# Cutting the last load before the first store into 16 KB runs, and the first store into a 16 KB and a 48 KB part

## Chip, cores and metric

One core of a Trainium2 chip. The metric is the device time of one execution in microseconds. Most executions of one kernel agree within about 0.3%, single ones lie further off; differences are therefore told as a ratio with a 95% interval, and "faster" or "slower" means by more than 2%.

## The reference

A rotary embedding on half of each head. `x` is (16, 512, 16, 64) in float32, 33.55 MB; the first 32 numbers of each head are rotated with tables `cos` and `sin`, the other 32 pass unchanged.

```python
x1, x2 = x[..., :32], x[..., 32:]
first  = x1[..., :16] * cos[..., :16] - x1[..., 16:] * sin[..., :16]
second = x1[..., :16] * sin[..., :16] + x1[..., 16:] * cos[..., :16]
return concatenate([first, second, x2], axis=-1)
```

The work is small; the 67.1 MB that must be read and written are the problem.

## The kernel before

`x` is seen as four tiles of 8 MiB. In each, a partition holds 16 rows of 4 KB, next to each other in memory, so that a transfer of n rows moves one run of n x 4 KB per partition. The profile counts 16 transfer engines, and each moves eight of the 128 runs of such a transfer. A ring of three tiles in the on-chip memory takes the loads; VectorE rotates in place; the store goes out from the ring.

```python
    def load(t, lo=0, hi=K):                      # K = 16 rows
        nc.sync.dma_start(out=rows(t, lo, hi), in_=xf[t, :, lo * R : hi * R])

    def store(t, lo=0, hi=K):
        nc.sync.dma_start(out=of[t, :, lo * R : hi * R], in_=rows(t, lo, hi))
    # ... stage is set to zero, cos and sin loaded from the GpSimd queue
    load(0, 0, K0)                                # K0 = 4
    load(0, K0, K)
    load(1)
    load(2, 0, KC)                                # KC = 8
    # ... the tables are spread over the partitions on VectorE
    rotate(0, 0, K0)
    rotate(0, K0, (K0 + K) // 2)
    rotate(0, (K0 + K) // 2, K)
    store(0)
    load(2, KC, K)
    load(3)                                       # its ring slot is that of tile 0
    for t in range(1, T):                         # T = 4
        rotate(t, 0, KC)
        rotate(t, KC, K)
        store(t)
```

All loads and stores are issued by the sync engine and stand in one queue. It turns from loading to storing twice: at the first store, and after the load of tile 3.

Of the kernel before, what the change touches and what calls it, by code (L numbers as in the profile page):

```python
# [1 line left out]

# [4 lines left out]


@with_exitstack
def kernel(  # L10
    ctx: ExitStack,
    tc: tile.TileContext,
    x: bass.AP,
    cos: bass.AP,
    sin: bass.AP,
    out: bass.AP,
):
    nc = tc.nc
    fp32 = mybir.dt.float32
    P = 128  # L20
    B, S, H, D = x.shape
    Q = D // 4
    HF = D // 2



    K = 16
    T = B * S // (P * K)
    PB = S // K
    REP = P // PB  # L30
    R = H * D
    NS = 3
    KC = K // 2
    K0 = K // 4

    xf = x.rearrange("b s h d -> (b s h d)").rearrange("(t p f) -> t p f", t=T, p=P)
    of = out.rearrange("b s h d -> (b s h d)").rearrange("(t p f) -> t p f", t=T, p=P)
    cosf = cos.rearrange("(p k) j -> p (k j)", k=K)
    sinf = sin.rearrange("(p k) j -> p (k j)", k=K)

    const_pool = ctx.enter_context(tc.tile_pool(name="const", bufs=1))
    b_pool = ctx.enter_context(tc.tile_pool(name="bp", bufs=1, space=bass.MemoryType.PSUM))


    ring = const_pool.tile([P, NS, K, H, D], fp32)
    stage = const_pool.tile([P, 2, K, HF], fp32)
    spun = const_pool.tile([P, 2 * K, Q], fp32)
    packed = const_pool.tile([PB, 2 * K, Q], fp32)
    table = const_pool.tile([P, 2, K, 2, Q], fp32)

    def rows(t, lo, hi):
        return ring[:, t % NS, lo:hi].rearrange("p k h d -> p (k h d)")

    def load(t, lo=0, hi=K):
# [6 lines that stand above are left out]
    nc.vector.memset(stage[:, :, :, 0:Q], 0.0)  # L61
    spread = stage.rearrange("(j b) t k i -> j b t (k i)", b=REP)
    nc.gpsimd.dma_start(out=spread[:, 0, 0], in_=cosf)  # L63
    nc.gpsimd.dma_start(out=spread[:, 0, 1], in_=sinf)  # L64
    load(0, 0, K0)
    load(0, K0, K)
    load(1)
    load(2, 0, KC)




    PQ = PB // REP
    nc.vector.stream_shuffle(  # L74
        out=spun[:],
        in_=stage.rearrange("p t k j -> p (t k) j")[:, :, 0:Q],
        mask=[j % PQ * REP for j in range(PB)],
    )
    for q in reversed(range(REP)):
        n = PQ * (q + 1)  # L80
        nc.vector.tensor_copy(out=packed[0:n], in_=spun[q * PB : q * PB + n])  # L81

    for r in range(REP):
        nc.vector.tensor_copy(  # L84
            out=table[r * PB : (r + 1) * PB].rearrange("p t k c j -> p (t k) c j"),
            in_=packed.unsqueeze(2).to_broadcast((PB, 2 * K, 2, Q)),
        )
    C = table[:, 0].rearrange("p k c j -> p k (c j)")
    Sn = table[:, 1].rearrange("p k c j -> p k (c j)")

    def rotate(t, lo, hi):
        n = hi - lo
        x1 = ring[:, t % NS, lo:hi, :, 0:HF]
        c = C[:, lo:hi].unsqueeze(2).to_broadcast((P, n, H, HF))
        s = Sn[:, lo:hi].unsqueeze(2).to_broadcast((P, n, H, HF))
        b_full = b_pool.tile([P, KC, H, HF], fp32, name="b_t")
        b_t = b_full[:, 0:n]
        nc.vector.tensor_mul(out=b_t, in0=x1, in1=s)  # L98
        nc.vector.tensor_mul(out=x1, in0=x1, in1=c)  # L99
        nc.vector.tensor_sub(  # L100
            out=x1[:, :, :, 0:Q], in0=x1[:, :, :, 0:Q], in1=b_t[:, :, :, Q:HF]
        )
        nc.vector.tensor_add(  # L103
            out=x1[:, :, :, Q:HF], in0=x1[:, :, :, Q:HF], in1=b_t[:, :, :, 0:Q]
        )

    rotate(0, 0, K0)
    rotate(0, K0, (K0 + K) // 2)
    rotate(0, (K0 + K) // 2, K)
    store(0)  # L110
    load(2, KC, K)
    load(3)
    for t in range(1, T):
# [5 lines that stand above are left out]
# [1 line left out]
_INS = ['x', 'cos', 'sin']  # L120
_OUTS = [((16, 512, 16, 64), 'float32')]


# [23 lines left out]
```

## Time and profile before

| | before |
|---|---|
| time, median of 3 runs | 162.55 us (162.5 to 162.89) |
| span of the profiled run | 160.9 us |
| VectorE busy | 112.9 us (70%) |
| transfer queue busy, of 16 engines' span | 97.7% |
| mean rate over the span | 418 GB/s |

The span is shorter than the time because the time also counts what is around the program. In the lines of the profile, DVE is VectorE, POOL is GpSimd, SPq is the sync engine's queue, and L55 is line 55 of the kernel. The row to look at is the queue: with 97.7% busy, only two things can be gained, the rest of 2.3%, or time in which packets move slowly though they count as busy. The second kind is not to be seen in a busy share.

### The profile page before, as it was taken

What the parts mean: (1) busy time and instruction counts of PE and PEld (TensorE: products, weight loads), DVE (VectorE), ACT (ScalarE), POOL (GpSimd) and SP (SyncE); (2) the same over time, 40 slices, a digit from 0 to 9 for tenths busy, and PEclk for the clock granted to TensorE, in tenths of its full rate; (3) what the DMA queues carried; (4) which work ended last, traced back from release to release, by engine and by line L of the source; (5) the groups of instructions that cost most, each with busy time, mean ns of one, the idle gap of its engine ahead of it and who ended that gap; (6) DMA issues with size and microseconds to landing.
All of it is one profiled execution on the core that took longest, in us unless ns stands there. A gap on an engine that the chain in (4) does not pass through costs nothing.

```text
span 160.9 us, 116 instructions
## 1 busy us (share of the span) xinstructions
DVE 112.9 (70%) x47; POOL 1.4 (1%) x6
## 2 busy tenths in 40 slices
DVE  1049999999999999999999991699999900000000
POOL 3000000000000000000000000000000000000000
DMA  6999999969999996999996996998998998998992
GB/s 195 554 391 391 391 456 521 521 261 521 391 391 261 521 521 261 521 391 391 472 570 261 521 521 261 521 423 358 521 423 358 521 423 358 521 423 358 521 423 98
DMA packets 1504, 67.24 MB, mean 418 GB/s; under 512 B 192, under 2 KB 192, under 8 KB 224
## 3 DMA queue, kind: packets, MB, share of 16 engines
q1 hardware_dynamic: 1440, 67.11, 97.7%
q0 software_dynamic: 64, 0.13, 0.2%
HBM read 33.69 MB, written 33.55 MB: 418 GB/s over the span
## 4 chain that ended last, share of the span: by engine, by line
DMA 50%; DVE 28%; DVEq 1%; issue 0%; SPq 0%
DMA ring<-in_x_dram 31%; DMA out_dram<-ring 18%; DVE b_t L98 10%; DVE ring L99 10%; DVE ring L100 5%; DVE ring L103 3%; DVEq L142 1%; SPq L55 0%; DVEq L98 0%
## 5 line engine op out<-in xcount | busy, mean ns | idle before, releaser
L98 DVE TENSOR_TENSOR b_t<-ring,table 128x4096 f32<-128x4096 f32 (+2 forms) x9 | 35.6, 3959 | 5.4 <-DMA ring<-in_x_dram 5.2
L99 DVE TENSOR_TENSOR ring<-ring,table 128x4096 f32<-128x4096 f32 (+2 forms) x9 | 35.6, 3950 | 0.3
L100 DVE TENSOR_TENSOR ring<-ring,b_t 128x2048 f32<-128x2048 f32 (+2 forms) x9 | 18.4, 2049 | 0.3
L103 DVE TENSOR_TENSOR ring<-ring,b_t 128x2048 f32<-128x2048 f32 (+2 forms) x9 | 18.4, 2042 | 0.0
L74 DVE LOAD_MASK_SELECT spun<-stage x1 | 0.0, 14 | 8.7 <-DMA stage<-in_sin_dram 8.7
L84 DVE COPY table<-packed 32x1024 f32<-32x1024 f32 x4 | 2.7, 684 | 0.1
L81 DVE COPY packed<-spun 32x512 f32<-32x512 f32 (+3 forms) x4 | 1.7, 416 | 0.1
L61 DVE MEMSET stage<- 128x512 f32 x1 | 0.5, 485 | 0.9 <-PEq L131 0.9
L74 DVE STREAM_SHUFFLE spun<-stage 128x512 f32<-128x512 f32 x1 | 0.7, 722 | 0.0
L63 POOL DMA_DIRECT2D stage<-in_cos_dram x1 | 0.6, 649 | 1.3 <-DVE stage L61 1.3
L64 POOL DMA_DIRECT2D stage<-in_sin_dram x1 | 0.5, 532 | 0.0
L131 POOL MEMSET const-bfloat16-1.0<- 128x1 bf16 x1 | 0.1, 96 | 0.0
L131 POOL MEMSET const-float32-0.0<- 128x1 f32 x1 | 0.1, 93 | 0.2 <-issue 0.2
L131 POOL MEMSET const-float32-1.0<- 128x1 f32 x1 | 0.1, 93 | 0.0
L131 POOL MEMSET const-uint8-127<- 128x1 uint8 x1 | 0.1, 93 | 0.0
## 6 DMA issues: line engine op xcount, KB each, us to landing
ring<-in_x_dram SPq DMA_DIRECT2D x2, 4096.0 KB, 44.9
ring<-in_x_dram SPq DMA_DIRECT2D x1, 6144.0 KB, 21.6
ring<-in_x_dram SPq DMA_DIRECT2D x1, 2048.0 KB, 7.7
stage<-in_cos_dram POOLq DMA_DIRECT2D x1, 64.0 KB, 6.3
stage<-in_sin_dram POOLq DMA_DIRECT2D x1, 64.0 KB, 7.7
out_dram<-ring SPq DMA_DIRECT2D x4, 37.2
ring<-in_x_dram SPq DMA_DIRECT2D x2, 34.7
```

Source lines behind the costliest of these rows:

```text
L61: nc.vector.memset(stage[:, :, :, 0:Q], 0.0)
L63: nc.gpsimd.dma_start(out=spread[:, 0, 0], in_=cosf)
L64: nc.gpsimd.dma_start(out=spread[:, 0, 1], in_=sinf)
L74: nc.vector.stream_shuffle(out=spun[:], in_=stage.rearrange("p t k j -> p (t k) j")[:, :, 0:Q], mask=[j % PQ * REP for j in range(PB)],)
L81: nc.vector.tensor_copy(out=packed[0:n], in_=spun[q * PB : q * PB + n])
L84: nc.vector.tensor_copy(out=table[r * PB : (r + 1) * PB].rearrange("p t k c j -> p (t k) c j"), in_=packed.unsqueeze(2).to_broadcast((PB, ...
L98: nc.vector.tensor_mul(out=b_t, in0=x1, in1=s)
L99: nc.vector.tensor_mul(out=x1, in0=x1, in1=c)
L100: nc.vector.tensor_sub(out=x1[:, :, :, 0:Q], in0=x1[:, :, :, 0:Q], in1=b_t[:, :, :, Q:HF])
L103: nc.vector.tensor_add(out=x1[:, :, :, Q:HF], in0=x1[:, :, :, Q:HF], in1=b_t[:, :, :, 0:Q])
L131: nc = _bacc.Bacc("TRN2", target_bir_lowering=False, num_devices=1)
L142: with _tile.TileContext(nc) as tc:
```

## The change

The intent: packets are slow only where the queue turns from loading to storing, so let the packets there be short.

```diff
-    load(2, 0, KC)
+    load(2, 0, K0)
+    load(2, K0, KC)
...
-    store(0)
+    store(0, 0, K0)
+    store(0, K0, K)
```

## The prediction

> **What bounds the kernel now.** I read the page first, for busy shares and the queue, then the chain of waits, then the timeline of issues, then the stretches around the places where the queue turns from loading to storing.
>
> From the page:
>
> ```profile
> span 160.9 us, 116 instructions
> DVE 112.9 (70%) x47; POOL 1.4 (1%) x6
> DMA  6999999969999996999996996998998998998992
> ...
> q1 hardware_dynamic: 1440, 67.11, 97.7%
> ...
> HBM read 33.69 MB, written 33.55 MB: 418 GB/s over the span
> ```
>
> The reader should see that VectorE has 30% to spare and the transfer queue has 2% to spare: its packets took 97.7% of what 16 engines have in 160.9 us. The sixes in the row of tenths are not idle time; a packet is booked where it starts, and one of 64 KB lasts longer than half a slice. The 67.11 MB cannot shrink, because the change neither adds nor drops a byte. So only two things in the queue can move the time: engine time that is idle, and engine time in which a packet moves slower than it could.
>
> The issues, from the timeline (start, length, queue, line):
>
> ```profile
> 0.74 1.89 SPq L55 DMA_DIRECT2D ring<-in_x_dram  x4
> 43.37 0.35 SPq L58 DMA_DIRECT2D out_dram<-ring  x1
> 43.77 29.60 SPq L55 DMA_DIRECT2D ring<-in_x_dram  x2
> 73.46 55.74 SPq L58 DMA_DIRECT2D out_dram<-ring  x3
> ```
>
> Four loads, 20 MiB, are queued at 0.74 us. The first store is issued at 43.37, while the fourth load is still moving, so there is no hole in front of it. The last store is issued at the end of the last stretch, 73.46 + 55.74 = 129.2, and it needs 8.39 MB / 435 GB/s = 19.3 us; as the queue ends near 159.6, its turn comes only at about 140. So VectorE is some 11 us ahead at the end. The chain view says the same in another way: it runs through VectorE up to 128.8 and stops there; its shares (DMA 50%, DVE 28%) are one path of releases and not what limits the rate.
>
> Now the rate, stretch by stretch (from and to, length, busy of VectorE and GpSimd, clock, DMA share, GB/s):
>
> ```profile
> 41.20:48.40 7.20, 7.13 (x4) 0.00 (x0) 1.00 1.01 437
> 48.40:52.40 4.00, 3.97 (x2) 0.00 (x0) 1.00 0.95 262
> 52.40:71.70 19.30, 19.16 (x7) 0.00 (x0) 1.00 1.00 435
> 71.70:81.40 9.70, 9.63 (x3) 0.00 (x0) 1.00 1.00 432
> 81.40:98.30 16.90, 15.62 (x6) 0.00 (x0) 1.00 1.00 434
> 98.30:101.00 2.70, 0.00 (x0) 0.00 (x0) 1.00 1.10 437
> 101.00:120.40 19.40, 18.27 (x6) 0.00 (x0) 1.00 1.01 439
> ```
>
> These are the first six of eight runs per engine of the fourth load (32 KB each), its last two, the first store, the second half of tile 2's load, seven of eight runs of the load of tile 3, its last run, and the second store. Everything goes at 432 to 439 GB/s, but the second line is at 262 with the engines at work for 0.95 of it. In that line 262 x 4.00 = 1048 KB moved, two 32 KB runs on each of 16 engines; they took 0.95 x 4.00 = 3.80 us where 1048 KB / 435 = 2.41 us would do. **The first turn from load to store costs 1.39 us**, in the last two runs of the load and not in the store. The single transfer records of the trace agree: a 32 KB run takes 1.213 us everywhere else, and there, averaged over the engines, the two together took 1.38 us more. At the second turn the line at 98.30 is 16 runs of 64 KB, one per engine, with 1.10 x 2.70 = 2.97 us of records begun in it, of which 0.3 belong to packets on its rim; the records give 0.25 us over 2.418. From store to load (71.70) nothing is lost. The rest of the 2%: about 0.64 us in the very first run, 0.33 us of small gaps while the two table loads pass, and about 3 us ahead of the first byte and after the last.
>
> **What the Trainium skill says.** "DMA: Bandwidth & Descriptors", section "Where 436 GB/s comes from", puts the ceiling at 16 ports x 32 B x 850 MHz = 435.2 GB/s. The trace agrees: 435 in the long store. So no run size can make the undisturbed stretches faster. The same page, section "Why small descriptors are slow (HBM only)", gives a fixed cost of about 3 cycles for each packet; the trace gives a little more for these long runs: 16 KB take 611 ns and 64 KB 2418 ns, so 2418 - 611 = 1807 ns for 48 KB, and 611 - 1807/3 = 9 ns fixed. The same page, section "Two DMAs through the same engine are not ordered", says that descriptors start in order but are pipelined, and that the read and the write side of an engine are separate queues. So while the last load runs are being written, the reads of the store behind them can already be under way; this fits where the loss lies, and is my best reason for it, though no run shows it yet. "SBUF — State Buffer", section "Who interferes with whom", says that a DMA never contends with a compute engine; the trace agrees so far that 32 KB and 64 KB runs hold their time beside a VectorE that is busy 99% (41.20 and 52.40).
>
> **The change part by part.** (1) The load of rows 0 to 7 of tile 2 becomes two transfers of rows 0 to 3 and 4 to 7. On each engine 8 runs of 32 KB become 16 of 16 KB: 8 more x 9 ns = 0.07 us. (2) The first store becomes rows 0 to 3 (8 runs of 16 KB per engine) and rows 4 to 15 (8 of 48 KB) for 8 of 64 KB: again 0.07 us. (3) Two more completion writes per engine at 9 ns, 0.02 us. All of it lies on the path, as the engines are busy to the end: +0.16 us in sum. (4) Issues: the small store needs the first quarter of tile 0 alone, so it may be issued when VectorE is done with that at 22.6 us, but it stands in the same rings behind 20 MiB of loads that end at about 52.8; nothing starts earlier. Two more issues of about 0.4 us on the sync queue fall where it waits anyway. (5) The load of tile 3 now waits for both store parts. They land together with the old end, near 73, and its data are next in the queue only at 81.4: 8 us of slack. VectorE's instructions and their order are the same; its wait of 4.86 us for tile 3 stays and costs nothing, as the 11 us above show. (6) The turn: its 1.39 us now meets 16 KB runs on both sides. That is the one term that can shrink, and the intent of the change.
>
> **The rivals.**
> A. The engine reads ahead by a number of runs. For it: the slow stretch begins on all engines with the last run but one (between 48.73 and 49.00), and at the second turn it is also a whole last run that is slow. Then with 16 KB runs it holds half the bytes and costs half: 1.39 / 2 = 0.70 saved, 0.16 paid, -0.54: 162.0. If it vanished nearly altogether, -1.2: 161.4.
> B. The engine reads ahead by bytes, or the loss is a one-time filling of its buffers at the first store. For it: the second turn, with 64 KB runs, costs 0.25 and not 2.8 us, against what A says of larger runs; two 32 KB runs and one of 64 KB are the same bytes. Then the loss stays, spread over three or four 16 KB runs, and only the 0.16 us are left: 162.7.
> C. VectorE's traffic sets it: it was busy at the first turn and idle (0.00) at the second. Against it stand the skill and the other busy stretches. It gives 162.7 too, as VectorE does the same work at that time.
> D. The earlier issue of the small store opens a hole, or the load of tile 3 is late, so that the store of 19.3 us is not covered. Slack of 8 us speaks against it; it would give 163 or more.
>
> **Range and chances.** B and C together get about 50%, A in its two forms 45%, D and anything unforeseen 5%. The first is at 162.7, the second at 161.4 to 162.0; the middle of this mixture is 162.3. Runs of the kernel before lie between 162.5 and 162.89, so 0.2 us of scatter is added on both sides: 161.4 to 163.0. Two per cent is 3.25 us, more than twice the whole loss at the turn, so faster than that is near impossible, and slower needs a hole in the queue: 1%, 98%, 1%.
>
> **What would show it right or wrong.** Right for A: in the stretch of the last 1 MB of loads before the first store, the changed kernel moves clearly more than 262 GB/s, with a loss of about 0.7 us, and the span is about 160.4. Right for B: about 1.4 us are lost there, over more runs. Everything else should stand still: 432 to 439 GB/s in the other stretches, a second turn of about 0.25 us, store to load without loss, VectorE's 112.9 us and its one wait near 102. I am wrong if the queue has a hole anywhere, if the loss moves to the border between the two store parts, or if the second turn changes along with the first.

## The result, and the profile after

| | before | changed |
|---|---|---|
| median of 4 runs each | 162.72 us (162.5 to 162.97) | 163.01 us (162.78 to 163.19) |
| ratio, 95% interval | | 1.0017 (0.9993 to 1.0041) |

A ratio is the mean time of one kernel's fast runs over that of the other's of the same rounds, so it is not quite the ratio of the medians. The median of 163.01 lies 0.01 above the top of the predicted range; carried to the 162.55 that the prediction started from, the ratio gives 162.83, which lies inside. The point of 162.3 was too low either way.

The page of the changed kernel:

```profile
span 160.6 us, 122 instructions
DVE 112.9 (70%) x47; POOL 1.4 (1%) x6
...
q1 hardware_dynamic: 1728, 67.11, 97.7%
```

VectorE and the share of the queue are as they were; the queue has 288 more packets, the 256 of the cut runs and 32 completion writes. The issues, in the timeline of the changed kernel:

```profile
0.74 2.38 SPq L55 DMA_DIRECT2D ring<-in_x_dram  x5
22.47 21.34 SPq L58 DMA_DIRECT2D out_dram<-ring  x2
43.85 29.36 SPq L55 DMA_DIRECT2D ring<-in_x_dram  x2
73.30 55.54 SPq L58 DMA_DIRECT2D out_dram<-ring  x3
```

The small store is issued at 22.47 us and not at 43.4, as foreseen, and nothing comes earlier for it. Then the rate by stretches of the changed kernel (columns as in the prediction: from and to, length, busy of VectorE and GpSimd, clock, DMA share, GB/s):

```profile
41.20:46.20 5.00, 4.97 (x3) 0.00 (x0) 1.00 0.98 419
46.20:48.40 2.20, 2.17 (x2) 0.00 (x0) 1.00 1.06 454
48.40:52.00 3.60, 3.60 (x1) 0.00 (x0) 1.00 0.96 287
52.00:71.30 19.30, 19.13 (x8) 0.00 (x0) 1.00 1.01 438
71.30:81.00 9.70, 9.63 (x3) 0.00 (x0) 1.00 1.00 432
97.80:100.40 2.60, 0.00 (x0) 0.00 (x0) 1.00 0.94 403
```

The slow stretch is still there, in the same place, with 16 KB runs in it. How much it costs is worked out from such a line in one way throughout this document: share x length is the engines' time for what began in the stretch, GB/s x length the bytes, and bytes / 435 GB/s the time that they need; the difference is the loss. Here 0.96 x 3.60 = 3.46 us for 1033 KB, which need 2.38: **1.08 us**, against 1.39 before. At the second turn it is 0.94 x 2.60 - 1048 / 435 = 0.03, against 0.26 (line 98.30:101.00 of before). The queue of this one trace is thus some 0.4 us shorter and the span 0.3 us, and yet the times do not fall. One of the two must be scatter, and the experiments begin there. (The traced execution was the fastest of the changed kernel's four: its span is 160.6 us, the others' are 160.7, 161.0 and 161.0.)

### The profile page after: what moved, and what is told of

It reads as the page before. It is cut to its first block, busy times and chain, and to the rows that moved or that the text cites. A ratio compares the mean times of both kernels' runs of the same rounds, so it can differ in the third digit from the quotient of the medians.

```text
span 160.6 us, 122 instructions
## 1 busy us (share of the span) xinstructions
DVE 112.9 (70%) x47; POOL 1.4 (1%) x6
## 3 DMA queue, kind: packets, MB, share of 16 engines
q1 hardware_dynamic: 1728, 67.11, 97.7%
## 4 chain that ended last, share of the span: by engine, by line
DMA 50%; DVE 28%; DVEq 1%; issue 0%; SPq 0%
DMA ring<-in_x_dram 31%; DMA out_dram<-ring 18%; DVE b_t L99 10%; DVE ring L100 10%; DVE ring L101 5%; DVE ring L104 3%; DVEq L144 1%; SPq L55 0%; DVEq L99 0%
```

## The experiments

Two theories were left, as the prediction names them. A: the engine reads ahead by a number of runs, so short runs at the turn make it cheap. B: the engine has to get ahead by a number of bytes once, at the first store, whatever the runs. C, VectorE's traffic as the cause, was the third.

| run | what was changed against before | first turn, us lost | later turns | time, ratio to before (95%) |
|---|---|---|---|---|
| (before) | | 1.39 | 0.26 | |
| e1 | nothing | 1.15 | 0.20* | one look: 162.78 against 162.92 |
| (changed) | the change | 1.08 | 0.03 | 1.0017 (0.9993 to 1.0041) |
| e2 | the change again | 1.14 | 0.17* | 1.0018 (0.9993 to 1.0042) |
| e3 | only the load cut | 1.22 | 0.17* | 0.9997 (0.9975 to 1.0019) |
| e4 | only the store cut | 1.31 | 0.32* | 1.0011 (0.9989 to 1.0033) |
| e5 | no rotations | 1.03 | 0.07* | one look: 162.38 against 162.61 |
| e6 | an early small store | 1.18 | 0.09, 0.03* | 1.0025 (1.0007 to 1.0043) |
| e7 | tile 2 loaded whole | 1.10 | 0.09* | 1.0545 (1.0529 to 1.0561) |
| e8 | 4 KB runs before the store | 0.95 | 0.03* | 1.0004 (0.9989 to 1.0019) |
| e9 | 512 B of zeros stored at the start | 1.19 | 0.19* | 1.0017 (1.0002 to 1.0032) |
| e12 | 2 KB of zeros after the first load | 0.30 | 0.36* | 0.9993 (0.9971 to 1.0014) |
| e10 | 4 KB of zeros after the first load | 0.03 | 0.01* | 1.0056 (1.0038 to 1.0074) |
| e11 | stores from a second queue | 1.28 | under 0.1 in all* | 1.1141 (1.1119 to 1.1163) |

Values with a star come from the records of single transfers in the trace (the mean over 16 engines of what a transfer took beyond the usual time of its size), the others from the lines quoted here. Where both were taken they agree within 0.1.

### Is the difference between the two traces one of the kernels?

e1, no edit:

> The unchanged kernel, for a second trace. If what the turns cost is a property of the kernel, the first turn from load to store costs 1.38 us per engine again and the second 0.25, within 0.1. If they wander by 0.3 us from run to run, the drop from 1.38 to 1.04 and from 0.25 to 0.04 that the changed kernel's trace shows is no effect of the change.

The stretch at the first turn, second trace of before:

```profile
48.30:52.30 4.00, 3.96 (x2) 0.00 (x0) 1.00 0.89 262
```

0.89 x 4.00 - 1048 / 435 = 1.15 us. So the same kernel shows 1.39 and 1.15: it wanders by 0.24, more than the 0.1 allowed for, and most of the drop to 1.08 is within this.

e2, the change again, with five rounds:

> The changed kernel again, with more rounds. If the trace is right that the queue itself is 0.4 us shorter (0.34 less at the first turn, 0.21 less at the second, 0.16 more for runs), the ratio is 0.997 to 0.999. If the times are right, 1.001 to 1.003.

```profile
48.00:52.00 4.00, 4.00 (x1) 0.00 (x0) 1.00 1.03 324
```

1.03 x 4.00 - 1296 / 435 = 1.14 us, the value of e1, which was traced on the same chip. The ratio is 1.0018 again, so the times were right and not the single trace. The interval holds 1; that the change costs anything at all is not shown.

### One part alone

e3:

```diff
-    load(2, 0, KC)
+    load(2, 0, K0)
+    load(2, K0, KC)
```

> Only the load in front of the store in 16 KB runs. If the engine reads ahead by runs of the load (A), this alone brings the first turn from 1.38 to about 0.7 to 1.0 us; the store keeps 64 KB runs. If it reads ahead by bytes (B), the first turn stays at 1.2 to 1.5. Fixed cost 0.08 us.

```profile
48.00:52.00 4.00, 4.00 (x1) 0.00 (x0) 1.00 1.03 315
```

1.03 x 4.00 - 1260 / 435 = 1.22 us: above what A allowed (1.0), at the lower edge of B.

e4:

```diff
-    store(0)
+    store(0, 0, K0)
+    store(0, K0, K)
```

> Only the store in 4 and 12 rows, the load keeps 32 KB runs. If the length of the store's runs that are read ahead sets the loss, the first turn falls below 1.1 us here and not in the run with the split load. If the load's runs set it, it stays at 1.38. Fixed cost 0.08 us.

```profile
48.30:52.30 4.00, 3.96 (x2) 0.00 (x0) 1.00 0.94 266
```

1.31 us, not below 1.1. Neither part does what it was made for, and they do not do it together.

### Is it VectorE, or the size of the runs?

e5 leaves out all `rotate` calls, so its result is wrong; the transfers and their order stay.

```diff
-    rotate(0, 0, K0)
-    rotate(0, K0, (K0 + K) // 2)
-    rotate(0, (K0 + K) // 2, K)
...
-        rotate(t, 0, KC)
-        rotate(t, KC, K)
```

> The kernel before without its rotations (a wrong result on purpose): the same transfers in the same order with VectorE idle from about 16 us on. If VectorE's traffic makes the first turn dear (C), its loss falls from 1.38 to 0.3 us or less. If the transfers alone make it (A or B), it stays at 1.2 to 1.5.

```profile
48.00:52.00 4.00, 0.00 (x0) 0.00 (x0) 1.00 0.86 262
52.00:71.30 19.30, 0.00 (x0) 0.00 (x0) 1.00 1.00 435
```

VectorE is at 0.00 and the turn still costs 1.03 us, a little under the forecast of 1.2 and near the lowest of the others; the store behind it runs at the same 435 GB/s. C falls as the main cause; a tenth or two from VectorE could not be told from scatter. The time, 162.38 us without any rotation, also shows how little VectorE has to do with it.

e8, very short runs:

```diff
-    load(2, 0, KC)
+    for r in range(KC):
+        load(2, r, r + 1)
```

> Rows 0 to 7 of tile 2 in eight loads of 4 KB runs before the first store. A by runs: the first turn costs under 0.4 us; the fixed cost is (64 - 8) runs x 9 ns = 0.5 us. B by bytes: 1.0 to 1.5 us over some ten runs.

```profile
48.50:52.20 3.70, 3.70 (x1) 0.00 (x0) 1.00 0.99 319
```

0.95 us, with runs an eighth as long as before. A's forecast of under 0.4 fails; B's 1.0 is missed by 0.05. The 0.5 us that 56 more runs per engine were to cost at 9 ns each would be a ratio of 1.003, which lies outside the measured 0.9989 to 1.0019.

e7, long runs:

```diff
-    load(2, 0, KC)
+    load(2)
...
-    load(2, KC, K)
```

> Tile 2 loaded in one piece before the first store, so the first turn is from 64 KB to 64 KB runs, as the second. A by runs: 2 to 2.8 us at the first turn, or 0.25 if long runs are cheap. B, one-time or by bytes: 1.2 to 1.5 us.

```profile
57.70:61.60 3.90, 3.87 (x2) 0.00 (x0) 1.00 0.90 269
...
139.00:148.80 9.80, 8.89 (x3) 0.00 (x0) 1.00 0.08 33
```

1.10 us with 64 KB runs, 0.1 under B's forecast. So the loss is the same within its scatter for runs of 4, 16, 32 and 64 KB, which is the end of A. That this kernel is 8.9 us slower was not foreseen and has another cause, in the second line: from 139.0 to 148.8 the engines stand still (share 0.08). The load of tile 3 is issued only at 82.06, when the first store has landed, and with no second half of tile 2 left to move in between, the store of tile 1 goes ahead of it; tile 3 lands some 19 us later, and VectorE is waited for at the end:

```profile
121.06 4.43 DVE L98 TENSOR_TENSOR b_t<-ring,table 128x4096 f32<-128x4096 f32 x1 [23.96 <-DMA ring<-in_x_dram]
```

VectorE waits 23.96 us where it waited 4.86 before. The half load behind the first store is what gives the kernel before its slack.

### Once, or at each turn?

e6 puts the 4-row store in front of tile 2's load, so that there are three turns:

```diff
-    load(2, 0, KC)
...
     rotate(0, 0, K0)
+    store(0, 0, K0)
+    load(2, 0, KC)
...
-    store(0)
+    store(0, K0, K)
```

> The 4-row store stands in the queue before tile 2's load, so there are three turns from load to store: 64 KB to 16 KB runs, then 32 KB to 48 KB, then 64 KB to 64 KB. If the loss is a one-time filling at the first store (B), the first of them costs 1.0 to 1.4 us and the second under 0.4. If every turn behind 32 KB runs costs it (A), the second costs 1.2 to 1.4 and the first under 0.4.

```profile
38.40:42.30 3.90, 3.87 (x3) 0.00 (x0) 1.00 0.92 269
...
53.20:56.90 3.70, 3.67 (x3) 0.00 (x0) 1.00 1.00 425
```

The first line is the last part of tile 1's load before the small store: 0.92 x 3.90 - 1049 / 435 = 1.18 us lost. The second is the end of the 32 KB runs before the 12-row store, the same runs that lost 1.39 before: now 3.70 - 1572 / 435 = 0.09. **Nearly all of the loss is paid once, at the first store.** This fits the cheap last turn of every kernel here too (0.01 to 0.36 us; why it is not always near 0 is not known). The time is 0.25% up, more than the one added transfer can explain; the one trace does not show where, and this stays open.

### Cold path, or bytes?

Paid once could still mean two things: something about the very first write, or a number of bytes to get ahead by. e9 stores 512 bytes of zeros per partition at the start, to a place that the first store overwrites later, so the result stays right:

```diff
+    blank = const_pool.tile([P, 128], fp32)
+    nc.gpsimd.memset(blank[:], 0.0)
+    nc.scalar.dma_start(out=of[0, :, 0:128], in_=blank[:])
     nc.vector.memset(stage[:, :, :, 0:Q], 0.0)
```

> Before anything else a store of 512 bytes of zeros per partition (64 KB in all) to the place that the first store overwrites later, from the scalar queue. If the loss belongs to the very first write to memory, whatever its size (cold path), the first full turn from load to store falls from 1.1-1.4 to under 0.3 us and the ratio is 0.993 to 0.997. If the engine has to get a fixed number of bytes ahead at the first turn, 8 runs of 512 bytes give it 4 KB of some 30 to 37 KB, the turn still costs 0.9 to 1.3 us, and the ratio is 0.999 to 1.003.

```profile
48.30:52.30 4.00, 4.00 (x1) 0.00 (x0) 1.00 0.90 262
```

1.19 us remain. The records show the zeros written between 4.1 and 9.9 us, so there had been a write to the output long before, and a cold first write is not it.

e10 makes the dose larger, 4 KB per partition or 32 KB per engine, between the first two loads (the zeros lie in a ring slot that is loaded later):

```diff
+    nc.vector.memset(ring[:, 2, 0], 0.0)
...
     load(0, 0, K0)
+    nc.sync.dma_start(out=of[0, :, 0:R], in_=rows(2, 0, 1))
     load(0, K0, K)
```

> The same with 4 KB runs (8 per engine, 32 KB) between the first two loads. Cold path: the loss of the turn moves here, and the later turns cost under 0.3 us each. Bytes ahead: 32 KB read while the first load is written costs up to 1.1 us here, and the first full turn falls to 0.3 us or less; if what was gained is lost again while loads run, it stays at 1.0 to 1.4. In all cases 8 x 156 ns = 1.25 us are added for the bytes themselves, so the ratio is 1.006 to 1.016.

```profile
1.70:8.30 6.60, 0.77 (x1) 1.18 (x2) 1.00 0.99 329
...
49.60:53.10 3.50, 3.46 (x2) 0.00 (x0) 1.00 1.02 440
53.10:72.40 19.30, 19.16 (x7) 0.00 (x0) 1.00 1.00 435
```

The start of before, for comparison:

```profile
1.70:7.50 5.80, 0.00 (x0) 1.18 (x2) 1.00 0.99 378
```

The end of the 32 KB runs before the first full store goes at 440 GB/s: the slow stretch is gone, 1.02 x 3.50 - 1540 / 435 = 0.03. It has been paid earlier instead: in the same working the start loses 0.99 x 6.60 - 2171 / 435 = 1.54 us, where it lost 0.99 x 5.80 - 2192 / 435 = 0.70 in before, so 0.84 more. (The records show the first 2 MB load complete at 8.45 to 9.04 us on the engines, where it was 7.50 to 7.88; of these 1.05 us a part may be table loads that pass in between.) The zeros take another 1.25, while some 1.5 are saved at the two turns (the mean of the two traces of before, 1.27 and 0.23). That is +0.6 to +0.8 in sum, and 0.56% of 162.59 is +0.9, with an interval from 0.6 to 1.2 (the ratio is under the 1.006 that was the least expected). It is no gain, but it moves the loss.

e12 halves the dose: 2 KB per partition, 16 KB per engine.

```diff
+    nc.vector.memset(rows(2, 0, 1)[:, 0 : R // 2], 0.0)
...
     load(0, 0, K0)
+    nc.sync.dma_start(out=of[0, :, 0 : R // 2], in_=rows(2, 0, 1)[:, 0 : R // 2])
     load(0, K0, K)
```

> As the run with 4 KB runs of zeros between the first two loads, but with 2 KB: 16 KB per engine instead of 32. If the loss is the time that it takes to read a number of bytes ahead once, and nothing else, half of the dose leaves about half: 0.4 to 0.8 us at the first full turn, where 4 KB left 1.2 and 32 KB left none. If some small dose opened a path, none is left; if 32 KB is a threshold, 1.1 to 1.3 are left. For the bytes 8 x 81 ns = 0.65 us are added, for reading ahead 0.3 to 0.6 at the early store, so the ratio is 1.001 to 1.006.

```profile
1.70:8.30 6.60, 0.24 (x1) 1.18 (x2) 1.00 0.98 344
...
49.00:52.40 3.40, 3.37 (x2) 0.00 (x0) 1.00 0.91 357
```

0.91 x 3.40 - 1214 / 435 = 0.30 us. So 4, 16 and 32 KB per engine leave 1.19, 0.30 and 0.03 us. The loss falls with the dose, neither at the first touch nor at a threshold of 32 KB; 0.30 is a little less than the half that was expected (0.4 to 0.8). What is gone has moved here too: the start loses 0.98 x 6.60 - 2270 / 435 = 1.25 us, 0.55 more than before, and 0.55 + 0.30 is about the 0.84 + 0.03 of e10. All three stores of zeros are eight runs per engine, so their bytes differ and not their number. The smallest dose is not quite of the series: in e9 the zeros came from another queue and in turn with the first loads.

The time is that of before (0.9993, at most 1.0014). The ratio lies under the 1.001 to 1.006 that was expected, and its interval under the sum of the trace: 0.55 more at the start and 0.65 for the zeros, 0.97 saved at the first turn, 0.13 more at the second, +0.36 us or 1.002. The traced execution was the slowest of the six (163.29 us), and the rest is not explained.

### Loads and stores side by side

e11 issues the stores from the scalar engine:

```diff
     def store(t, lo=0, hi=K):
-        nc.sync.dma_start(out=of[t, :, lo * R : hi * R], in_=rows(t, lo, hi))
+        nc.scalar.dma_start(out=of[t, :, lo * R : hi * R], in_=rows(t, lo, hi))
```

> The kernel before with its stores issued on the scalar queue, so that loads and stores take turns on each engine and there is no single turn. If the loss is one-time, 1.0 to 1.4 us are lost where stores first meet loads and no more later, and the ratio is 0.997 to 1.01. If every change of direction with loads pending costs something, the rate while both queues are at work falls clearly under 432 GB/s and the ratio is above 1.02.

```profile
43.40:48.20 4.80, 4.76 (x2) 0.00 (x0) 1.00 1.02 328
...
43.00:135.00 92.00, 58.13 (x18) 0.00 (x0) 1.00 1.01 433
135.00:150.00 15.00, 14.88 (x5) 0.00 (x0) 1.00 0.16 70
```

The ratio of 1.114 would speak for a cost at each change of direction, but the rate does not. The first line covers the last three load runs per engine in front of the first store run, of which two are slow: 1.02 x 4.80 - 1574 / 435 = 1.28 us lost. From there to 127 us the records show that the engines pass from load runs to store runs and back more than 30 times, and every run takes its usual 1.213 or 2.418 us; from 43 to 135 us they move 433 GB/s on average. So this run too, and more clearly than e6, shows the loss once and then no more. It also shows where it lies: the two slow runs are the fourth and fifth of the eight of their load, so what counts is that the first store run comes next, and not that a load ends.

The ratio that was forecast for a loss paid once (0.997 to 1.01) is missed for another reason. The time goes in 135 to 150, where the engines are idle (share 0.16): the loads share the engines with stores, tile 3 lands late (its first rotation waits 25.2 us), and the last store has to wait for VectorE. It is the same hole as in e7, got in another way.

No run beats the kernel before.

## Why the prediction was right, point by point

**The range: kept, but with little test in it.** It was wide enough for A, B and C alike, so that the time alone says nothing of the mechanism. Its ends are also not what its sum gives: with 0.2 us added on both sides, 161.4 and 162.7 make 161.2 and 162.9, and not 161.4 and 163.0.

**What bounds the kernel: right.** The queue is at 97.7% in both kernels, VectorE at 112.9 us in both, and without any rotation the time is 162.38.

**The loss at the first turn: right in place, less sure in size.** 1.39 us was read from one trace, and is the highest of all. The twelve traces other than e10 and e12 give 0.95 to 1.39, and two of the same kernel give 1.39 and 1.15. A difference of 0.3 between two traces is no finding here. One sign that the prediction named for being wrong did show: in the first trace of the changed kernel the second turn fell along with the first, from 0.26 to 0.03. The second traces (0.20 in e1, 0.17 in e2) make that scatter as well.

**Fixed cost of the cut runs: too high, and too small to matter.** The prediction took 9 ns for each more run, +0.16 us. In the records of before, consecutive transfers of one engine overlap by about 4 ns: 16 KB runs follow one another every 607.4 ns and 64 KB runs every 2414.1. So 48 KB take 1806.7 ns, a run costs 607.4 - 1806.7 / 3 = about 5 ns, and 18 more of them 0.09 us. The measured +0.17% is 0.28 us, with an interval from -0.1 to +0.7: it holds both and shows neither.

**Issues, slack, VectorE: right.** The small store is issued at 22.47 us, no hole opens, the long store moves at 438 GB/s across the border between its parts, and the last stores keep their slack.

**The rivals.** B was right, in its one-time form: e6 and e11 show that it is paid once, e12 and e10 that bytes count. A, to which the prediction gave 45%, fell. Its argument was that the slow stretch begins with the last run but one on all engines; but that was two 32 KB runs by chance of size. In the changed kernel the slow stretch covers about the last three 16 KB runs, and in e7 the last 64 KB run. What the prediction held against A, the cheap second turn behind 64 KB runs, was the better evidence, and should have had more weight: with B alone the point would have been 162.7 and not 162.3. C fell with e5, D did not happen.

**What stays open.** That the read side of an engine runs ahead into the store's data while its write side still writes the load is the picture that the prediction drew, and the runs fit it: paid once, by bytes, without VectorE, in the last load runs and not in the store. It is argued and not shown; no record tells reads from writes. A write path that needs some tens of KB per engine to come up to speed would fit the doses of e9, e12 and e10 as well, though less well the place of the loss, in load runs; no run parts the two. Why the loss scatters between 0.95 and 1.39, why up to 0.36 us remain at the second turn, and what e6 pays its 0.25% for, is open too.

## What to carry to other kernels

A full queue can hide slow packets, so read the rate by stretches and not only the busy share; then, before cutting anything at a slow place, ask if it comes again at the next place of the same kind: here the second turn, in the same trace, had already spoken against run size as the cause. A loss of under 1% that two traces of the same kernel put at 1.39 and 1.15 us can't be tuned on single traces. And a transfer that looks as if it could go earlier (half of tile 2, e7) may be the one that keeps the queue fed while the next load waits for a store to land.

## What the Trainium skill lacked or had wrong

- "DMA: Bandwidth & Descriptors" has no word on a loss when a queue turns from loads to its first stores. The runs show 0.95 to 1.39 us at the first store, whatever the runs (4 to 64 KB), 0.01 to 0.36 us at a later turn, and 0.03 us at the first full store after 32 KB per engine had been stored early. In e11 loads and stores taking turns run by run moved 433 GB/s over 92 us.
- The same page, section "Why small descriptors are slow (HBM only)", gives about 3 cycles for each packet. For runs of 16 to 64 KB the trace shows about 5 ns net for each, which is some 4 cycles at the 850 MHz that the page states (an estimate from these two): the right size, a little low.
- The same page, section "Rules for kernel authors", says that spreading transfers over issuing engines does not help and only saves issue time. It does not say that it can harm: with the stores on a second queue, the order between loads and stores was lost and the time rose from 162.59 to 181.25 us, by an idle stretch and not by a lower rate.
